# A run of 1,596 extra TensorE products ahead of a decoder step on one core

## The chip, the cores and the metric

One core of a Trainium2 chip runs the whole program. Its engines work side by side and meet at semaphores: TensorE multiplies (PE in the profile, its weight loads PEld), VectorE (DVE) and ScalarE (ACT) do what is elementwise, GpSimd (POOL) a few small things, and SyncE (SP) issues nearly all DMAs. The metric is the device time in microseconds of one execution; lower is better.

## The reference

One layer of a decoder step, for a prompt of 256 tokens and 8 samples of 4 tokens, 288 tokens in all, with a model width of 2048. Everything is in float32.

```python
def _layer(x, c, conv_prefix, chunk, ...):
    mod = (jax.nn.silu(c) @ w_ada + b_ada).reshape(n, N_MOD, 1, D_MODEL)
    sh_m, sc_m, gt_m, sh_f, sc_f, gt_f = [mod[:, i] for i in range(N_MOD)]
    h = _rms(x, g_mix) * (1 + sc_m) + sh_m
    proj = h @ w_in
    b_gate, c_gate, hc, u, v, ga, gb = jnp.split(proj, idx, axis=-1)
    ...
    merged = jax.nn.sigmoid(ga) * (ya @ w_pa) + jax.nn.sigmoid(gb) * (yb @ w_pb)
    x = x + gt_m * (merged @ w_out)
    h2 = _rms(x, g_ffn) * (1 + sc_f) + sh_f
    gate, up = jnp.split(h2 @ w_ffn_in, 2, axis=-1)
    x = x + gt_f * ((jax.nn.silu(gate) * up) @ w_ffn_out)
```

The first product is the conditioning, `silu(c) @ w_ada`; the large ones are those with `w_in`, `w_pa`, `w_pb`, `w_out`, `w_ffn_in` and `w_ffn_out`. The result is `x` under a last norm, with some states of the mixers.

## The kernel before

**Tiles.** Features lie on the 128 partitions and the 288 tokens along a row, so a product has a weight tile of 128x128 as the operand that is loaded and 288 columns (298 for some early ones) that stream through. The output takes the first 288 of the 512 columns of one bank of PSUM. Four banks are called `main` (the names `pm`), three `misc` (`px`), one `ada`.

**Three products for one.** Each float32 operand is split into a high part, rounded to the type FP32R, and a low part, what is left. `triple` (L236) multiplies high by high (L239), high by low (L242) and low by high (L244, or L241 in another order) into one sum. Each product has a weight load of its own in the trace. Weights are split on arrival, the high part on ScalarE (L480), the low one on VectorE (L487, or L258 where the planner of the head does it). The columns that stream through are cut from `slots`, whose FP32R tiles begin seven elements into their buffer (`LEADIN`). The plain FP32 products are those of the conditioning (L412), the sums of squares (L213), the transposes and the spatial mixing.

**Fillers.** `warm(n)` (L600 to L604) multiplies a BF16 tile of ones, `wb`, into the bank `idle`, 288 columns wide, n times; no result is read.

**Order.** TensorE's instructions run in the order in which the Python code calls them. In the head of the program the same holds for ScalarE, VectorE and SyncE. The steps run from a list: 19 fillers, the first conditioning block `a0` (two loads, with 5 fillers between them and 6 inside), then `first_tile`, which makes the first tile of activations out of them (VectorE's L426, L709 and L711, ScalarE's L710), 2 and 6 fillers beside it, then the products of `w0` (L534, L536, L542 and on), with the second conditioning block `a1` among them (L412 again).

**Loads.** All large loads go through one pool of seven buffers, `raw` (`RAW = 7`), in turn: a load waits until what was in its buffer seven loads ago has been read. SyncE issues them in order, at the head `a0`, `w0` and a slice of `x`, `a1`, a slice of `x`, `wK`, `wA` and more of `x`.

Of the kernel before, what the change touches and what calls it, by code (L numbers as in the profile page):

```python
# [8 lines left out]
F32 = mybir.dt.float32  # L9
F32R = mybir.dt.float32r  # L10
# [4 lines left out]
P = 128  # L15
D = 2048
T = 288
# [10 lines left out]
RAW = 7  # L28
# [60 lines left out]
def decoder_kernel(tc, d):  # L89
    nc = tc.nc  # L90
    from contextlib import ExitStack

    with ExitStack() as es:
        def pool(name, bufs=1, **kw):
            return es.enter_context(tc.tile_pool(name=name, bufs=bufs, **kw))

        pc = pool("const")
        pw = pool("wstream")
        pslot = pool("slots", MAIN)
        pkept = pool("kept", KEPT)  # L100
        ptmp = pool("tmp", 5)
        pps = pool("psum", 4, space=bass.MemoryType.PSUM)
        with tc.manual_schedule(engines={nc.tensor.engine}):
            _body(tc, nc, d, pc, pw, pslot, pkept, ptmp, pps)


def _body(tc, nc, d, pc, pw, pslot, pkept, ptmp, pps):
    ids = [0]

    def nm(s):  # L110
        ids[0] += 1
        return f"{s}_{ids[0]}"

    def const(name, shape, dt=F32):
        return pc.tile(shape, dt, tag=name, name=name)
# [12 lines left out]
    def psmain():  # L128
        return pps.tile([P, 512], F32, tag="main", name=nm("pm"), bufs=4)
# [4 lines left out]
    V, A, G, PE, SY = nc.vector, nc.scalar, nc.gpsimd, nc.tensor, nc.sync  # L134
# [16 lines left out]
    x = const("x", [P, 16, T])  # L151
# [215 lines left out]
    class Step:  # L367
        defer = apart = False
        raw = None
# [227 lines left out]
    wb = const("wb", [P, 288], BF16)  # L597
    G.memset(wb, 1.0)
    idle = psmain()
# [200 lines left out]
    def sinkD(m, ps):  # L800
        a = part[m]
        V.tensor_tensor(a, ps[:, :T], a, ALU.add)  # L802
        if 32 <= m < 40:
            gelu2(a)
            if m == 32:
                S["accv"] = SquareSum()
            S["accv"].add(a)
        elif 24 <= m < 32:
            gelu2(a)
            u2[m - 24] = a  # L810
        elif m >= 40:
            A.activation(a, a, AF.Tanh, scale=0.5)
        elif m >= 16:
            mix_conv(m - 16)
# [283 lines left out]
        tail.close()  # L1098


    rh1 = h1.__getitem__
    def at(main, plan):
        out, n = [], 0
        for s in main:
            out.append(s)
            if isinstance(s, Blk):
                n += 1
                out += plan.pop(n, [])
        assert not plan
        return out  # L1110
# [32 lines left out]
    def wD(m0, m1):  # L1143
        return [Blk("wD", i, rh1, sinkD) for i in range(m0 // 2, m1 // 2)]

    first = [Half(n, 0, rh1, lambda j, ps: sinkD(32 + j, ps)) for n in ("wE", "wF")] + wD(36, 40)
# [47 lines left out]
    n = len(steps)  # L1194
# [30 lines left out]
    for s in steps:  # L1225
# [14 lines left out]
        i = pos[id(s)]  # L1240
# [124 lines left out]
```

## Time and profile before

| | |
|---|---|
| median of 2 runs | 1593.24 us (1593.21 to 1593.26) |
| the profiled execution's own time | 1593.33 us |
| its span, first to last instruction | 1591.5 us |
| mean granted TensorE clock | 0.998 of full |
| DMA share of the 16 engines, 0 to 20 and 20 to 40 us | 0.93 and 1.02 |

Times in the trace count from the first instruction. A row of the timeline has the start, the duration, the engine, the line, the operation, what it writes and reads, the shape (128*128 is the weight tile, 128x288 what streams through) and how many alike were merged; in brackets stands the idle time ahead and what ended it. A group's row ends with busy time, the mean of one in ns, and the idle time ahead of the group. A row of the windows has for each engine the busy time and, in brackets, the records that lie in the stretch. TensorE's records overlap: the mean of one says how long it is under way, while the distance from start to start says what it costs.

### The profile page before, as it was taken

The page shows a single profiled execution, that of the slowest core. Times are in us where ns is not written, and L with a number is a line of the kernel's source. Part 1 is how long each engine was busy: PE and PEld are TensorE (multiplying, and loading weights), DVE is VectorE, ACT ScalarE, POOL GpSimd, SP SyncE. Part 2 cuts the span into 40 slices and gives each one's busy share as a digit, 9 for nine tenths or more (in the row PEclk, how much of TensorE's full clock was granted, in tenths as well). Part 3 has the DMA queues.
Part 4 walks back from the last instruction along what each step waited for, and adds up shares of the span by engine and source line. Part 5 has one row for each costly group of instructions (what it writes and reads, how often), then busy time and mean ns, then how long its engine had stood idle before and what let it go on. Part 6 is the DMA issues. An engine that isn't in the chain of part 4 may idle for free.

```text
span 1591.5 us, 31811 instructions
## 1 busy us (share of the span) xinstructions
PE 1581.3 (99%) x12700; PEld 1520.3 (96%) x12700; DVE 1013.9 (64%) x2200; ACT 735.7 (46%) x1366; POOL 21.4 (1%) x65
## 2 busy tenths in 40 slices
PE   9999999999999999999999999999999999999997
PEld 8998999998999989899898999999999999999997
DVE  6676788877755658567844555555555555555565
ACT  6633344643444435356643444444444444444464
POOL 0000000000001000011000000000000000000000
PEclk9999999999999999999999999999999999999999
DMA  9887866777767778784757356453464534645341
GB/s 381 333 322 288 320 243 217 283 280 305 283 232 263 312 290 267 269 295 169 293 180 277 128 182 212 159 177 111 170 232 159 175 121 164 230 159 176 112 165 60
DMA packets 67541, 357.89 MB, mean 225 GB/s; under 512 B 7616, under 2 KB 19264, under 8 KB 37696
## 3 DMA queue, kind: packets, MB, share of 16 engines
q1 hardware_dynamic: 67104, 355.73, 61.2%
q8 instruction: 99, 1.62, 0.4%
q14 instruction: 50, 0.41, 0.1%
q10 hardware_dynamic: 288, 0.13, 0.0%
HBM read 352.74 MB, written 3.09 MB: 224 GB/s over the span
## 4 chain that ended last, share of the span: by engine, by line
PE 99%; DVE 1%; ACT 0%; DVEq 0%; issue 0%; POOL 0%; POOLq 0%
PE pm L239 31%; PE pm L244 30%; PE pm L242 30%; PE ada L412 5%; PE pm L604 0%; DVE st L1079 0%; PE px L242 0%; PE px L239 0%; PE px L244 0%; PE px L213 0%; PE px L911 0%; PE px L910 0%; PE px L857 0%; PE px L1051 0%; PE pm L241 0%; DVE q L620 0%
## 5 line engine op out<-in xcount | busy, mean ns | idle before, releaser
L239 PE MATMUL pm<-s,hi 128*128 128x288 f32 (+1 forms) x3750 | 1095.1, 292 | 0.0
L242 PE MATMUL pm<-s,hi 128*128 128x288 f32 (+1 forms) x3750 | 1090.6, 291 | 0.0
L244 PE MATMUL pm<-s,lo 128*128 128x288 f32 (+1 forms) x3738 | 1088.1, 291 | 0.0
L480 ACT CAST hi<-raw 128x512 fp32r<-128x512 f32 (+1 forms) x963 | 585.2, 610 | 776.8 <-PE pm L242 730.9
L487 DVE TENSOR_TENSOR lo<-raw,hi 128x512 fp32r<-128x512 f32 (+1 forms) x849 | 577.3, 682 | 409.7 <-ACT hi L480 397.6
L239 PEld LDWEIGHTS pm<-s,hi 128*128 128x128 f32 x3750 | 702.1, 187 | 12.7 <-issue 10.4
L242 PEld LDWEIGHTS pm<-s,hi 128*128 128x128 f32 x3750 | 702.2, 187 | 0.1
L244 PEld LDWEIGHTS pm<-s,lo 128*128 128x128 f32 x3738 | 699.9, 187 | 0.0
L258 DVE TENSOR_TENSOR lo<-raw,hi 128x512 fp32r<-128x512 f32 x111 | 74.6, 676 | 28.3 <-ACT hi L480 27.5
L412 PE MATMUL ada<-raw,cs 128*32 128x512 f32 (+2 forms) x1088 | 81.0, 445 | 0.0
L412 PEld LDWEIGHTS ada<-raw,cs 128*32 128x32 f32 x1088 | 29.2, 110 | 40.6 <-issue 37.9
L802 DVE TENSOR_TENSOR s<-pm,s 128x288 f32<-128x288 f32 x72 | 32.8, 456 | 16.6 <-PE pm L244 16.4
L311 ACT CAST s<-t 128x288 fp32r<-128x288 f32 (+1 forms) x76 | 32.9, 433 | 15.4 <-DVE t L834 9.1
L313 DVE TENSOR_TENSOR s<-t,s 128x288 fp32r<-128x288 f32 (+1 forms) x76 | 35.0, 460 | 6.0 <-ACT s L311 5.2
L353 DVE SCALAR_TENSOR_TENSOR x<-pm,mod,x 128x256 f32<-128x256 f32 x79 | 37.5, 475 | 0.0
L1000 DVE SCALAR_TENSOR_TENSOR t<-t,pm 128x288 f32<-128x288 f32 x42 | 19.1, 454 | 19.6 <-PE pm L244 19.6
L794 DVE TENSOR_TENSOR s<-pm,s 128x288 f32<-128x288 f32 x48 | 21.8, 454 | 9.9 <-PE pm L244 9.1
L352 DVE TENSOR_TENSOR t<-pm,mod 128x32 f32<-128x32 f32 x79 | 15.1, 192 | 20.0 <-PE pm L244 19.5
L785 DVE TENSOR_TENSOR s<-s,rb 128x288 f32<-128x288 f32 x48 | 21.6, 449 | 0.0
L181 ACT ACTIVATE t<-x 128x288 f32<-128x288 f32 x29 | 12.9, 444 | 17.7 <-DVE x L356 17.7
L186 DVE TENSOR_TENSOR acc<-acc,t 128x288 f32<-128x288 f32 x33 | 15.0, 455 | 8.2 <-ACT t L181 8.2
L779 DVE SCALAR_TENSOR_TENSOR s<-pm,s 128x256 f32<-128x256 f32 x36 | 17.3, 481 | 2.7 <-PE pm L244 2.7
(170 smaller groups left out, 489.5 us busy)
## 6 DMA issues: line engine op xcount, KB each, us to landing
raw<-in_fi SPq DMA_DIRECT2D x84, 1024.0 KB, 4.8
raw<-in_a SPq DMA_DIRECT2D x56, 1024.0 KB, 4.9
raw<-in_f SPq DMA_DIRECT2D x64, 704.0 KB, 3.9
raw<-in_wD SPq DMA_DIRECT2D x34, 1024.0 KB, 6.9
raw<-in_aE SPq DMA_DIRECT2D x16, 1024.0 KB, 9.6
raw<-in_wo SPq DMA_DIRECT2D x16, 1024.0 KB, 5.7
raw<-in_wC SPq DMA_DIRECT2D x19, 768.0 KB, 4.4
raw<-in_pa SPq DMA_DIRECT2D x8, 1024.0 KB, 9.8
```

Source lines behind the costliest of these rows:

```text
L239: PE.matmul(out, wh, ah, start=first, stop=False)
L242: end_ = PE.matmul(out, wh, al, start=False, stop=turn and last)
L244: end_ = PE.matmul(out, wl, ah, start=False, stop=last)
L258: lows.pop(0)[1]()
L311: A.copy(hi, a)
L313: V.tensor_tensor(lo, a, hi.bitcast(F32), ALU.subtract)
L353: V.scalar_tensor_tensor(x[:, m, :TP], ps[:, :TP], mod[:, gt0 + m, 0:1], x[:, m, :TP], ALU.mult, ALU.add)
L412: PE.matmul(acc[32 * j : 32 * j + 32, h * w // n : (h + 1) * w // n], cs[:, kt, :], self.held[2 * j + h] if self.held else self.raw[:, o : ...
L480: A.copy(hi, self.raw[:, s * 128 : e * 128])
L487: sub()
L794: return V.tensor_tensor(part[m], ps[:, :T], part[m], ALU.add)
L802: V.tensor_tensor(a, ps[:, :T], a, ALU.add)
```

## The change

A function `bench` is added and called once, ahead of the list of steps. VectorE fills a tile of 2048 columns with 0.75; VectorE copies it to one FP32R tile and ScalarE to two more. The four tiles come from the pool of the stream buffers. TensorE then runs 48 fillers and 516 times three products of these constants. They go to `idle` and to three more banks of `main`, and nothing reads them: four times into each bank in turn; to 56 places of one bank (columns 0, 4, ... 220) and to four more (2, 6, 10, 14), six times each; in five orders of banks and places, eight times each, once each product starting its sum and once each adding to what is there; and at nine widths from 288 to 240 columns, eight times each. The columns that stream begin at element 23 or 535 of their tile; the weights begin at multiples of 128 elements, for the low part with 40 added.

```diff
+    def bench():
+        f = pw.tile([P, 2048], F32, tag="raw", name=nm("bench"), bufs=RAW)
+        V.memset(f, 0.75)
+        rs = []
+        for i in range(3):
+            r = pw.tile([P, 2048], F32R, tag="raw", name=nm("benchr"), bufs=RAW)
+            A.copy(r, f) if i else V.tensor_copy(r, f)
+            rs.append(r)
+        r0, r1, r2 = rs
+        outs = [idle] + [psmain() for _ in range(3)]
+
+        def triple_(i, o, out, n=T, first=True):
+            a, b = r2[:, 23 : 23 + n], r2[:, 535 : 535 + n]
+            w, l = (r[:, s + P * (i % 8) : s + P * (i % 8) + P] for r, s in ((r0, 0), (r1, 40)))
+            for q, (x, y) in enumerate(((w, a), (w, b), (l, a))):
+                PE.matmul(out(q)[:, o : o + n], x, y, start=first, stop=True, skip_group_check=True)
+
+        def one(k):
+            return lambda q: outs[k]
+
+        for i in range(48):
+            PE.matmul(idle[:, :T], wb[:, :P], wb, start=True, stop=True)
+        for i in range(4):
+            triple_(i, 0, one(i))
+        for o in range(0, 224, 4):
+            for i in range(6):
+                triple_(i, o, one(0))
+        for o in (2, 6, 10, 14):
+            for i in range(6):
+                triple_(i, o, one(0))
+        for first in (True, False):
+            for i in range(8):
+                triple_(i, 0, one(0), first=first)
+            for i in range(8):
+                triple_(i, 0, one(i % 4), first=first)
+            for i in range(8):
+                triple_(i, 0, lambda q: outs[q], first=first)
+            for i in range(8):
+                triple_(i, 0, lambda q: outs[q % 2], first=first)
+            for i in range(8):
+                triple_(i, 224 * (i % 2), one(0), first=first)
+        for n in (288, 284, 280, 276, 272, 264, 256, 248, 240):
+            for i in range(8):
+                triple_(i, 0, one(0), n)
+
+    bench()
```

On TensorE the new products stand ahead of the 19 fillers with which its program began. This is the start of the changed program's products, behind the last of the 48 fillers (`pm_100` is `idle`; `benchr_103`, `_105` and `_107` are the three FP32R tiles; x2 is two products alike):

```order
L1122 MATMUL pm_100<-wb 128x288
L1116 MATMUL pm_100<-benchr_107,benchr_103 128x288 x2
L1116 MATMUL pm_100<-benchr_107,benchr_105 128x288
L1116 MATMUL pm_109<-benchr_107,benchr_103 128x288 x2
L1116 MATMUL pm_109<-benchr_107,benchr_105 128x288
L1116 MATMUL pm_110<-benchr_107,benchr_103 128x288 x2
L1116 MATMUL pm_110<-benchr_107,benchr_105 128x288
L1116 MATMUL pm_111<-benchr_107,benchr_103 128x288 x2
L1116 MATMUL pm_111<-benchr_107,benchr_105 128x288
```

Nothing stood there before. On ScalarE, whose copies these products wait for, the head of the program before:

```order
L138 DMA t_75<-in_c 128x144
L140 DMA cp_77<-in_cpack 128x112
L164 ACT_TABLE_LOAD
L164 ACTIVATE t_87<-t_75 128x144
L480 CAST hi_244<-raw_109 128x512
L710 ACTIVATE s_251<-x,gm_92 128x256
```

and now:

```order
L138 DMA t_75<-in_c 128x144
L140 DMA cp_77<-in_cpack 128x112
L164 ACT_TABLE_LOAD
L164 ACTIVATE t_87<-t_75 128x144
L1107 CAST benchr_105<-bench_101 128x2048
L1107 CAST benchr_107<-bench_101 128x2048
L480 CAST hi_1851<-raw_1716 128x512
L710 ACTIVATE s_1858<-x,gm_92 128x256
```

The two copies of constants stand between the start of the conditioning and the first split of `w0`. On SyncE, the loads from the rest of `w0` on, before (in brackets the semaphores that a load waits for; those named DMAHW are earlier loads, and `raw_115` and `raw_118` are the two halves of `a1`):

```order
L461 DMA raw_109<-in_w 128x512 [waits DMAHW2_49]
L385 DMA raw_115<-in_a 128x1024 [waits DMAHW3_49]
L385 DMA raw_115<-in_a 128x1024 [waits DMAHW4_49]
L385 DMA raw_118<-in_a 128x1024 [waits DMAHW5_49]
L385 DMA raw_118<-in_a 128x1024 [waits DMAHW6_49]
L155 DMA x<-in_x 128x288 [waits DMAHW7_49]
L463 DMA raw_122<-in_wK 128x768 [waits DMAHW0_49]
```

and now:

```order
L461 DMA raw_1716<-in_w 128x512 [waits DMAHW2_49]
L385 DMA raw_1722<-in_a 128x1024 [waits DMAHW3_49,DVE_49,Activation_49]
L385 DMA raw_1722<-in_a 128x1024 [waits DMAHW4_49]
L385 DMA raw_1725<-in_a 128x1024 [waits DMAHW5_49,PE_49]
L385 DMA raw_1725<-in_a 128x1024 [waits DMAHW6_49]
L155 DMA x<-in_x 128x288 [waits DMAHW7_49]
L463 DMA raw_1729<-in_wK 128x768 [waits DMAHW0_49,PE_49]
```

The first half of `a1` now waits for the copies to have read the float32 constants, the second half and `wK` for TensorE to have read the FP32R ones.

## The prediction

> **What bounds the kernel now.** I read the page first: the shares of the engines, the slices, the chain that ended last. Then the windows, for the spacing of the products, and the timeline of the first 22 us, where the new work is put.
>
> ```profile
> span 1591.5 us, 31811 instructions
> PE 1581.3 (99%) x12700; PEld 1520.3 (96%) x12700; DVE 1013.9 (64%) x2200; ACT 735.7 (46%) x1366; POOL 21.4 (1%) x65
> PEclk9999999999999999999999999999999999999999
> PE 99%; DVE 1%; ACT 0%; DVEq 0%; issue 0%; POOL 0%; POOLq 0%
> ```
>
> TensorE is busy for 99% of the span, its granted clock is full in all forty slices, and 99% of the chain of waits is TensorE itself. So the test for any added work is whether it is on TensorE. What a product costs is its spacing, start to start, since the records overlap. The windows give it for a stretch that holds little else than products 288 wide, and the timeline gives it for 298 columns and for the BF16 fillers.
>
> ```profile
> 1300.00:1580.00 280.00, 280.00 (x2164) 280.00 (x2162) 161.76 (x328) 133.02 (x239) 0.00 (x0) 1.00 0.43 148
> ...
> 12.72 0.29 PE L239 MATMUL px<-s,hi 128*128 128x298 f32 x1
> ...
> 14.59 0.29 PE L242 MATMUL pm<-s,hi 128*128 128x298 f32 x1
> ...
> 1.13 4.74 PE L604 MATMUL pm<-wb 128*128 128x288 bf16 x19 [1.13 <-POOL wb L598]
> 5.80 1.24 PE L412 MATMUL ada<-raw,cs 128*32 128x64 f32 x64
> 6.97 0.79 PE L604 MATMUL pm<-wb 128*128 128x288 bf16 x5
> ...
> 9.70 1.15 PE L604 MATMUL pm<-wb 128*128 128x288 bf16 x8
> 11.01 0.40 PE L534 MATMUL pm<-s,hi 128*128 128x298 f32 x1 [0.16 <-ACT s L710]
> ...
> L239 PE MATMUL pm<-s,hi 128*128 128x288 f32 x3626 | 1058.0, 292 | 0.0
> ...
> L604 PE MATMUL pm<-wb 128*128 128x288 bf16 x49 | 9.6, 348 | 1.1 <-POOL wb L598 1.1
> ```
>
> 280 us hold 2164 products, of which two straddle the edges: 280/2162 = 0.1295 us each. Between 12.72 and 14.59 us lie 14 steps of 298-wide products: 1.87/14 = 0.1336 us. Ten columns more cost 4.1 ns, so 0.41 ns a column: the width sets the spacing there, on a fixed part of 129.5 - 288 x 0.41 = 11 ns. A merged row of n records lasts n - 1 spacings and one record, and the groups give the record (292 ns for a product, 348 on average for a filler, near 290 for one at full speed). So the first 19 fillers are spaced (4.74 - 0.35)/18 = 0.244 us, the last 8 (1.15 - 0.29)/7 = 0.123 us: TensorE starts at half speed and has reached full speed by the row at 6.97, whose five are spaced (0.79 - 0.29)/4 = 0.125 us.
>
> **What the change adds on TensorE.** 48 fillers and, from `triple_`, three products a call. The calls: 4 that touch each of four banks, 56 places x 6, 4 places x 6, two passes of five orders x 8, and nine widths x 8: 4 + 336 + 24 + 80 + 72 = 516 calls, 1548 products. Of these 9 x 8 x 3 = 216 belong to the widths, and 1332 are 288 wide. Nothing can hide them: TensorE runs in program order, they stand ahead of everything, and no other engine ends the span.
>
> The 288-wide ones are the kernel's own product in shape and type, with the same two weights for three streams (high, high, low), and the L239 rows stand for them. Sum: 1332 x 0.1295 = 172.5 us.
>
> The 216 narrower ones have 288, 284, 280, 276, 272, 264, 256, 248 and 240 columns, 24 each, 267.6 on average. By 0.41 ns a column that is 129.5 - 20.4 x 0.41 = 121.1 ns, 26.2 us in all. No FP32R row of this trace is narrower than 288. The other end, no gain from narrowness, is 216 x 0.1295 = 28.0 us. A floor from the weight loads shows in the products of one column:
>
> ```profile
> 41.31 0.83 PE L213 MATMUL px<-ones,q 128*128 128x1 f32 x6 [0.20 <-DVE q L620]
> ...
> 426.89 0.60 PE L857 MATMUL px<-cp,s 128*128 128x128 f32 x4
> ...
> L857 PE MATMUL px<-cp,s 128*128 128x128 f32 x16 | 2.4, 272 | 0.0
> ...
> L213 PE MATMUL px<-ones,q 128*128 128x1 f32 x6 | 0.8, 254 | 0.2 <-DVE q L620 0.2
> ```
>
> Six products of one column take 0.83 us, (0.83 - 0.26)/5 = 0.114 us apart, where one column would need next to nothing: a new set of 128 weights is not taken faster than about 0.11 us. The line through the two widths meets that near 245 columns, so only the 240s could touch it, for a few ns on 24 products. I take 26.2 us.
>
> **The place in the bank and the order of the banks.** No row writes 288 columns anywhere but at a bank's start. The nearest is L857: four products that write at columns 0, 128, 256 and 384 of one bank stand (0.60 - 0.27)/3 = 0.11 us apart, each as the next. I price the place at nothing. Above, 1,086 products lie off the start, and if such a place cost what ten columns cost (4.1 ns), that is 4.5 us. Below, if it brought the spacing down to that of the BF16 fillers (0.123), 1,086 x 6.5 ns = 7 us less. For the order of banks the four L534, four L536 and four L542 change bank with every product, the first four starting a sum, the others adding; this group gives the spacing:
>
> ```profile
> 11.65 0.69 PE L536 MATMUL pm<-s,lo 128*128 128x298 f32 x4
> 12.19 0.69 PE L542 MATMUL pm<-s,hi 128*128 128x298 f32 x4
> ```
>
> (0.69 - 0.29)/3 = 0.133 us in both, the 298-wide spacing within one bank. So the five orders, adding or overwriting, cost nothing extra.
>
> [...]
>
> **When they start, and the head behind them.** The operands are constants: a VectorE memset of 2048 columns, one VectorE copy, two ScalarE copies.
>
> ```profile
> 4.67 0.32 ACT L164 ACTIVATE t<-t 128x144 f32<-128x144 f32 x1 [1.72 <-DMA t<-in_c]
> ...
> L480 ACT CAST hi<-raw 128x512 fp32r<-128x512 f32 x892 | 549.4, 618 | 714.4 <-PE pm L242 673.0 <-PE pm L244 10.4 <-DVE lo L487 6.6
> ...
> L480 ACT CAST hi<-raw 128x256 fp32r<-128x256 f32 x5 | 2.0, 407 | 1.6 <-DVE s L785 0.9 <-PE pm L242 0.6
> ```
>
> ScalarE's queue holds them behind L164, which waits for a DMA to 4.67 and ends at 4.99. 512 columns take 618 ns, 256 take 407: 0.82 ns a column, so 2048 take 1.88 us, and two are done at 8.8. VectorE's memset and copy are done before that, and what they push back there (L165 and L166, wanted at 5.80 before) is now wanted only 200 us later. Meanwhile TensorE runs the 48 fillers: 21 at 0.244 from 1.13 to some 6.2, then 27 at 0.123, to 9.5. So the first product starts at about 9.6, held by the fillers rather than by ScalarE, and the last ends at 9.6 + 172.5 + 26.2 = 208.3.
>
> Behind it stands the old head, unchanged: 19 fillers, now at full speed, 19 x 0.123 = 2.3 us with 0.1 for the change of type, and then what took from 5.80 to 11.01 before, 5.2 us, less 0.1 as its first 64 products ran partly at half speed. L534 comes at 208.3 + 2.4 + 5.1 = 215.8 in place of 11.01. What follows keeps its order. The shift is 204.8 us.
>
> **The loads that wait.** Four of the seven stream buffers now hold the constants, so the second half of `a1` and all behind it on SP's queue (a slice of x, `wK`, `wA`) issue only at 208.3, when the last product has read its operands. Before:
>
> ```profile
> 6.65 2.88 SPq L385 DMA_DIRECT2D raw<-in_a  x4
> 9.63 0.37 SPq L155 DMA_DIRECT2D x<-in_x  x1
> 10.28 0.33 SPq L463 DMA_DIRECT2D raw<-in_wK  x1
> ...
> 17.31 1.15 PE L412 MATMUL ada<-raw,cs 128*32 128x64 f32 x64
> ...
> 19.13 0.51 ACT L480 CAST hi<-raw 128x384 fp32r<-128x384 f32 x1 [3.63 <-DVE gm L709]
> ```
>
> That half of `a1` is the last two of the four at 6.65, some 8.3, 2.7 us ahead of L534; now it is 7.5 us ahead. It is wanted at 17.31, 6.3 behind L534, so 13.8 us after its issue; `wK` is wanted at 19.13, 8.1 behind L534, so some 14 after its own. A DMA of `a1` takes 6.9 us to land, one of `wA`, the slowest at the head, 10.0:
>
> ```profile
> raw<-in_a SPq DMA_DIRECT2D x8, 512.0 KB, 6.9
> raw<-in_wA SPq DMA_DIRECT2D x6, 512.0 KB, 10.0
> ```
>
> So I cost this at nothing: the cover is the head's 7.5 us. Without it up to 8 us would show. The earlier loads (`a0`, `w0`, half of `a1`) land under the products, yet TensorE gains little, as it stood still for only parts of a microsecond between 11 and 40 us.
>
> **Sum.** The profiled execution took 1593.33 us, 1.83 more than its span, and the median is 1593.24, 0.09 less. 1591.5 + 204.8 = 1796.3 for the span, and 1798.1 for the time; I say 1798.0.
>
> **Rivals.**
> - Narrow FP32R products run as plain FP32 ones, below a width that this trace doesn't show. A plain FP32 product leaves two records (L911, eight products, 16 records):
>
> ```profile
> L911 PE MATMUL px<-s,s 128*128 128x128 f32 x16 | 3.1, 275 | 0.0
> ...
> 287.17 4.50 PE L412 MATMUL ada<-raw,cs 128*32 128x512 f32 x40
> ...
> L412 PE MATMUL ada<-raw,cs 128*32 128x512 f32 x576 | 64.7, 594 | 0.0
> ```
>
>   At 512 columns four such records lie side by side, so 40 take ten steps: (4.50 - 0.59)/9 = 0.434 us, 0.85 ns a column. Two records of 244 columns are 0.415 us, against 0.112: 0.3 us more on each product concerned. If that is the two narrowest widths, 48 products, 14.5 us, which makes 1812.5. Against it: nothing in this trace hints at such a width; for it: the nine widths go well below what the kernel uses. Chance 0.09.
> - The FP32R products, freed of other engines' traffic, space as the BF16 fillers, 0.1225: 187.8 in place of 198.7, so 1787. Against it: the 0.1295 is as steady in the quiet stretch from 1300 to 1580 as elsewhere. 0.05. [...]
> - The loads behind the products don't come in time, or a place in the bank costs: 3 to 8 us, 1801 to 1806. 0.05.
> - TensorE's clock drops under the dense stream: at 0.244 a product 1548 x 0.115 = 178 us more, 1976. The kernel is itself such a stream at full clock; 0.01.
> - The other side, no slower: the products never run, since no result is read. They stand in the program as built, and the records of before hold 49 fillers (L604), whose results are not read either. With fillers and copies alone L534 would come at 17 and the time at 1599. It decides as soon as fewer than 32/0.13 = 246 of the 1548 are left. 0.01.
>
> **How the numbers follow.** The forecast has 0.79: 1798, and 1793 to 1803 by its own terms (the width's two ends, the place, a clock that rises 1.5 us earlier or later). 1790 to 1813 takes in the stall and the narrow rival and leaves out the BF16 spacing, the clock and the removal. 2% of the time, 32 us, is about what a measurement can tell from no change; all cases but the last lie far beyond it: slower 0.98, same 0.01, faster 0.01.
>
> **What would show it.** L1116 with 1548 records (a few per cent may be missing) and a spacing of 0.1295 at all 60 places and in all ten orders; widths that fall by 0.41 ns a column and flatten near 0.11; the first L1116 at 9.6, L534 at 216; `a1`'s second half issued when L1116 ends, and TensorE not waiting for it; the rest a copy of before. Wrong would be: a group of L1116 with another spacing, two records to a narrow product, or waits for a DMA in the 30 us behind.

## The result, and the profile after

The changed kernel takes 1797.51 us (1797.15 to 1797.87), against 1593.24: a ratio of 1.1282, 95% interval 1.1264 to 1.1300, so 204.3 us slower. The forecast was 1798.0.

The page of the changed kernel shows the same picture as before with one group more. The columns of the fifth row are shares of the chain that ended last, by engine and line:

```profile
span 1795.4 us, 35011 instructions
PE 1785.4 (99%) x14296; PEld 1723.4 (96%) x14296; DVE 1018.0 (57%) x2202; ACT 739.5 (41%) x1368; POOL 20.8 (1%) x65
PEclk9999999999999999999999999999999999999999
DMA  2000398786577767777766663554446443554341
PE pm L239 27%; PE pm L244 27%; PE pm L242 27%; PE pm L1116 11%; PE ada L412 5%; PE pm L604 0%; DVE st L1079 0%; DMA t<-in_c 0%; ACT benchr L1107 0%; PE px L242 0%; PE px L239 0%; PE px L244 0%; PE px L213 0%; PE px L911 0%; PE px L910 0%; PE px L857 0%
```

TensorE has 14296 - 12700 = 1596 records more, just the 48 fillers and 1,548 products: none was dropped, and none was run as two. The span and TensorE's busy time are both some 204 us longer. The DMA row shows three of forty slices without any traffic: those are the loads that waited for the products to end.

The timeline of the changed kernel, TensorE alone, at the start and the end of the new part:

```profile
8.87 71.31 PE L1116 MATMUL pm<-benchr,benchr 128*128 128x288 f32 x548
...
208.01 2.50 PE L604 MATMUL pm<-wb 128*128 128x288 bf16 x19
210.44 1.10 PE L412 MATMUL ada<-raw,cs 128*32 128x64 f32 x64
...
215.51 0.80 PE L534 MATMUL pm<-s,hi 128*128 128x298 f32 x4 [0.16 <-ACT s L710]
```

The new products take 208.01 - 8.87 = 199.1 us, L534 comes at 215.51 instead of 11.01, and what follows it lasts 1795.4 - 215.5 = 1579.9 us (before 1591.5 - 11.0 = 1580.5).

What each place, order and width costs is read from the same timeline in stretches that lie within one kind. A row gives the start, the duration of all, and their number; the spacing is the duration less one record (0.29 us at 288 columns), by the number less one. First a stretch of 536 products at places from column 0 on, then the four places 2, 6, 10 and 14, then the five orders that start a sum each time, then the five that add:

```profile
10.54 69.64 PE L1116 MATMUL pm<-benchr,benchr 128*128 128x288 f32 x536
...
141.08 9.49 PE L1116 MATMUL pm<-benchr,benchr 128*128 128x288 f32 x72
150.41 15.85 PE L1116 MATMUL pm<-benchr,benchr 128*128 128x288 f32 x121
165.97 15.72 PE L1116 MATMUL pm<-benchr,benchr 128*128 128x288 f32 x120
```

The spacings are 0.1296, 0.1296, 0.1297 and 0.1297 us. By the start times of the single products, each of the 60 places has 0.1296 to 0.1297 and each of the ten orders 0.1295 to 0.1297. So neither the place in a bank, nor the change of banks, nor adding in place of starting a sum has a price. The widths:

```profile
184.76 3.13 PE L1116 MATMUL pm<-benchr,benchr 128*128 128x284 f32 x23
193.93 3.02 PE L1116 MATMUL pm<-benchr,benchr 128*128 128x272 f32 x23
199.90 2.75 PE L1116 MATMUL pm<-benchr,benchr 128*128 128x256 f32 x22
205.43 2.52 PE L1116 MATMUL pm<-benchr,benchr 128*128 128x240 f32 x21
```

With records of 0.29, 0.29, 0.28 and 0.27 us that is 0.129, 0.124, 0.118 and 0.112 us: falling with the width, the last at the floor that the prediction read from the one-column products.

### The profile page after: what moved, and what is told of

Its sections match the earlier page's. It is cut to its first block, busy times and chain, and to the rows that moved or that the text cites. A ratio compares the mean times of both kernels' runs of the same rounds, so it can differ in the third digit from the quotient of the medians.

```text
span 1795.4 us, 35011 instructions
## 1 busy us (share of the span) xinstructions
PE 1785.4 (99%) x14296; PEld 1723.4 (96%) x14296; DVE 1018.0 (57%) x2202; ACT 739.5 (41%) x1368; POOL 20.8 (1%) x65
## 4 chain that ended last, share of the span: by engine, by line
PE 99%; DVE 1%; ACT 0%; DMA 0%; DVEq 0%; issue 0%
PE pm L239 27%; PE pm L244 27%; PE pm L242 27%; PE pm L1116 11%; PE ada L412 5%; PE pm L604 0%; DVE st L1079 0%; DMA t<-in_c 0%; ACT benchr L1107 0%; PE px L242 0%; PE px L239 0%; PE px L244 0%; PE px L213 0%; PE px L911 0%; PE px L910 0%; PE px L857 0%
## 5 line engine op out<-in xcount | busy, mean ns | idle before, releaser
L1116 PEld LDWEIGHTS pm<-benchr,benchr 128*128 128x128 f32 x1548 | 199.1, 187 | 0.4 <-ACT benchr L1107 0.4
L1116 PE MATMUL pm<-benchr,benchr 128*128 128x288 f32 (+7 forms) x1548 | 199.3, 290 | 0.1
L426 DVE STREAM_TRANSPOSE ev<-ada 128x512 f32<-128x512 f32 (+2 forms) x9 | 4.8, 537 | 225.6 <-PE ada L412 225.6
L412 PE MATMUL ada<-raw,cs 128*32 128x512 f32 (+2 forms) x1088 | 80.7, 444 | 0.0
L412 PEld LDWEIGHTS ada<-raw,cs 128*32 128x32 f32 x1088 | 29.0, 110 | 40.4 <-issue 38.1
```

The lines of the kernel that those rows point to most:

```text
L412: PE.matmul(acc[32 * j : 32 * j + 32, h * w // n : (h + 1) * w // n], cs[:, kt, :], self.held[2 * j + h] if self.held else self.raw[:, o : ...
L1116: PE.matmul(out(q)[:, o : o + n], x, y, start=first, stop=True, skip_group_check=True)
```

## The experiments

Each is an edit of the changed kernel. Where a kernel was timed, a time of the kernel before stood beside it, 1593.2 to 1593.3.

**What the products alone cost.** All but three of them are left out:

```diff
-        for i in range(4):
-            triple_(i, 0, one(i))
...
+        for k, r in enumerate(rs):
+            PE.matmul(outs[k + 1][:, :T], r0[:, :P], r[:, 23 : 23 + T], start=True, stop=True)
```

> Left out: the 1,548 products of constants but three, one for each tile; the 48 fillers, the copies and the four buffers stay. Theory (the time is the products' spacing, 199.0 us from 8.87 to 207.9, and a start of some 6 us): the products run from 8.87 to 9.3, 19 fillers follow for 2.4 us, L534 comes near 16.9 in place of 11.0, and the time is near 1599, so that the 1,545 products alone are worth 198 to 199 us. Rival (the held loads or the buffers taken cost something of their own, that hid in the 204 us): over 1602.

It took 1599.27 us (1598.90 to 1600.05). The 1,545 products are worth 1797.51 - 1599.27 = 198.2 us, as expected, and fillers, copies and taken buffers 6.0 us. In this execution full speed came later, 6.3 us into the span in place of 4.5, so the 48 fillers ran to 9.7 in place of 8.8, and L534 came at 17.42.

**What the fillers ahead of them do.** The 48 are left out:

```diff
-        for i in range(48):
-            PE.matmul(idle[:, :T], wb[:, :P], wb, start=True, stop=True)
```

> Left out: the 48 fillers ahead of the products. In the changed kernel the first product waits for ScalarE's copies to 8.87, 0.38 us behind the last filler. Theory: it still starts at 8.87, but at half speed, with a spacing of 0.24 us until the clock is granted in full some 3.5 to 5 us later; that costs 1.7 to 2.5 us, so about 1799.5. Rival (the fillers and not the copies hold the start, the clock does not matter here): the same time within 0.5 us or less.

It took 1799.48 us (1799.32 to 1799.64), 2.0 more. TensorE's timeline of this kernel at the start:

```profile
8.65 5.17 PE L1116 MATMUL pm<-benchr,benchr 128*128 128x288 f32 x20 [8.65 <-ACT benchr L1107]
13.83 5.36 PE L1116 MATMUL pm<-benchr,benchr 128*128 128x288 f32 x40
```

The first 20 products are (5.17 - 0.29)/19 = 0.257 us apart, the next 40 0.130. The start is ScalarE's, with and without fillers; what the fillers buy is full speed at that moment, 0.130 us in place of 0.257.

**Whether the held loads cost anything.** The constants lie in slots instead of stream buffers:

```diff
-        f = pw.tile([P, 2048], F32, tag="raw", name=nm("bench"), bufs=RAW)
+        f = tmp()
...
+        a, b = slot(F32R), slot(F32R)
+        w, l = (
+            pslot.tile([P, o + 256], F32R, tag="s", name=nm("s"), padded_shape=[P, PITCH])[:, o:] for o in (0, 8)
+        )
```

> The constants lie in four tiles of the activation slots in place of four stream buffers, so that no load waits for the products and all seven buffers are filled long before the first conditioning product. The weights repeat after two tiles in place of eight; everything else of the products is the same. Theory (the loads held behind the products were covered by the 7.5 us of the head): the smaller copies end before the fillers, the first product comes 0.3 us earlier, and the time is 1797.0, within 1 us of the changed kernel. Rival (TensorE waited for loads behind the products): 3 to 8 us faster, 1790 to 1794.

It took 1798.18 us (1798.14 to 1798.21), 0.7 more than the changed kernel, where 0.5 less was expected: a small miss, and on the side away from the rival. The first product came at 8.92, not earlier, since the fillers lasted that long in this execution, and the products themselves took 0.5 us longer from their other places. The loads, all there ahead of time, brought nothing, so in the changed kernel they cost nothing.

**How wide the cover is.** The prediction called the head's 7.5 us, from the last product to L534, the cover of the held loads. Of the fillers behind the products, the 30 in front of and within `a0` are left out:

```diff
-    a0[1].half = lambda: warm(6)
...
-    steps = [Do(lambda: warm(19)), a0[0], Do(lambda: warm(5)), a0[1]]
+    steps = [a0[0], a0[1]]
```

> Left out: the fillers of the old head that follow the products, 19 ahead of the first conditioning block, 5 ahead of its second load and 6 in it. Theory: they cost 30 times 0.123 us and some changes of type, about 4 us, and the held loads still come in time, as the second half of a1 is wanted some 9.7 us behind its issue in place of 13.5: 1793.5. Rival (these fillers cover the held loads): under 1.5 us gained, and TensorE waits for a DMA in the 20 us behind L534.

The two executions took 1794.48 and 1798.81 us. In the profiled one, which is the faster, L534 came 4.1 us earlier, as expected, but TensorE lost 1.2 us behind it. The same kernel again:

> The same kernel as the one without the old head's fillers, to see which of its two times holds. Theory (the 1.2 us in which TensorE stood still in the midst of the second a1 block are the price of going into the crowded loads early, and the slower execution had one more stretch at half speed): most runs near 1794.5, the idle time ahead of L412 there again. Rival (that idle time was chance): 1793.3 and no such idle time.

Four executions took 1794.77, 1796.81, 1796.88 and 1798.47 us. The expected idle time ahead of L412 was there again; "most runs near 1794.5" was a miss, with one of four there. TensorE's timeline and then the windows of this second profile (the last three columns of a windows' row are the granted clock, the DMA share and GB/s):

```profile
218.03 0.98 PE L412 MATMUL ada<-raw,cs 128*32 128x64 f32 x54
220.87 0.47 PE L412 MATMUL ada<-raw,cs 128*32 128x64 f32 x10 [1.86 <-issue]
221.28 0.62 PE L239 MATMUL pm<-s,hi 128*128 128x298 f32 x1
221.69 0.45 PE L241 MATMUL pm<-s,lo 128*128 128x298 f32 x1
```

```profile
212.00:219.00 7.00, 7.00 (x154) 6.42 (x153) 4.49 (x12) 3.61 (x10) 0.00 (x0) 1.00 0.98 321
219.00:221.10 2.10, 0.24 (x12) 0.23 (x10) 0.00 (x0) 0.00 (x0) 0.00 (x0) 1.00 1.02 413
221.10:224.50 3.40, 3.40 (x23) 3.25 (x15) 2.53 (x11) 1.43 (x3) 0.00 (x0) 0.50 1.02 415
```

TensorE stands still for 1.86 us after 54 of the 64 products of the second `a1` block, while the DMA engines are full (1.02). Just then the granted clock falls to 0.50 for 3.4 us: the pause costs 1.86 us for itself, and behind it products of 298 columns start 0.25 us apart, where the changed kernel has 0.13. It is not the block's own data, since each half of the block has its load and the second half begins with the 33rd product.

**Whether the crowded loads make that pause.** Both edits together, the constants in the slots and the fillers left out:

> Both edits together: constants in the activation slots, so that no load waits for the products, and none of the 30 fillers behind them. Theory (TensorE stood still in the midst of the second a1 block because the held loads crowded the DMA engines there): no idle time ahead of L412, the whole 4.1 us gained on the kernel with the slots, 1794.0. Rival (the idle time belongs to the short fillers being gone, whatever the loads do): about 1795.3, idle time there again.

It took 1793.85 us (1793.33 to 1793.98), four executions, and the block runs through:

```profile
218.42 1.10 PE L412 MATMUL ada<-raw,cs 128*32 128x64 f32 x64
219.45 0.40 PE L239 MATMUL pm<-s,hi 128*128 128x298 f32 x1
```

From 212 to 219 us the DMA share is 0.16 here, where it was 0.98 to 1.00 in the two profiles with the pause. So the pause comes from the loads that were held and then all issued at once.

What TensorE lacked in it, the waits don't name ("issue": no semaphore), but the trace's DMA packets point at its instructions. On the queue that the page calls instruction (q8), packets of 16 KB follow one another under the added products about every 16.6 us, the time of 128 products, so they look like TensorE's program. Both profiles with the pause stop ahead of the same product, the 55th. The last such packet before it came from 217.32 to 218.23 us for the pause that ended at 219.79, and from 218.54 to 219.49 for the one that ended at 220.87. With both edits it came from 215.24 to 216.56, well ahead of that product at 219.18. That the crowded DMA engines delayed TensorE's instructions fits all three profiles, but no experiment changed that alone.

**What sets a product's spacing: the width and the type.** Other widths, then BF16 and plain FP32 operands, in place of the places and orders:

```diff
+        for n in (512, 448, 384, 352, 320, 304, 288, 240, 224, 192, 128, 64):
+            for i in range(8):
+                triple_(i, 0, one(0), n)
```

> In place of the places and orders: FP32R products of 512 to 64 columns, 24 of each width, then BF16 products of 512, 288, 240 and 128 columns, 24 each, then plain FP32 ones of 512 and 288. Theory A (a fixed part of some 9.5 ns for each FP32R product, and a floor of the weight loads near 112 ns): 512 columns every 222 to 223 ns, 384 every 169, 224 to 64 every 112. Theory B (the extra lies in weight loads that hardly fit under 288 columns, and goes away where there is room): 512 columns every 216 ns as BF16, 384 every 162.5, and the same floor. Rival (narrow FP32R products run as plain FP32 ones): 224 to 64 columns cost more than 240. BF16: 216, 122.5, 102.5 and 56 ns if a product's columns set it, not under about 110 if the weight loads do. The whole time is no measure here.

TensorE's timeline of this kernel, FP32R (L1116) and BF16 (L1132):

```profile
12.93 5.26 PE L1116 MATMUL pm<-benchr,benchr 128*128 128x512 f32 x22
23.52 4.00 PE L1116 MATMUL pm<-benchr,benchr 128*128 128x384 f32 x22
...
44.10 2.51 PE L1116 MATMUL pm<-benchr,benchr 128*128 128x224 f32 x21
...
52.07 2.40 PE L1116 MATMUL pm<-benchr,benchr 128*128 128x64 f32 x20
...
61.52 2.86 PE L1132 MATMUL pm<-benchb 128*128 128x288 bf16 x22
64.46 2.42 PE L1132 MATMUL pm<-benchb 128*128 128x240 bf16 x22
66.92 1.34 PE L1132 MATMUL pm<-benchb 128*128 128x128 bf16 x21
```

A record takes 0.39 us at 512 columns, 0.33 at 384 and 0.27 to 0.28 at 224 and 64; of BF16 it takes 0.286 at 288, 0.266 at 240 and 0.22 at 128. So FP32R has 512 columns every 0.232 us, 384 every 0.174, 224 and 64 every 0.112, and BF16 288 every 0.1226, 240 every 0.1026, 128 every 0.056. BF16's 512 columns come every 0.216 us by their start times, once the clock, at half from 54.7 to 58.1 us, is full again. The rival of two records is gone: under 240 columns nothing doubles, and the spacing is flat near the 0.11 us that the prediction took for the weight loads. The price that it gave that rival was right: a plain FP32 product leaves two records in this run, 0.2425 us apart at 288 columns. Neither A (0.222) nor B (0.216) has the 512 right: what an FP32R product takes beyond BF16's spacing grows with its columns, from 7 ns at 288 to some 16 at 512.

**Whether the start of the columns plays a part.** 288 columns from other starts, and weights from others:

```diff
+        for at in (*range(0, 17), 20, 23, 24, 28, 31):
+            for i in range(8):
+                triple_(i, at, 0, 40)
```

> In place of the places and orders: 288-wide FP32R products, 24 each, whose columns begin at elements 0 to 16, 20, 23, 24, 28 and 31 of their tile, and whose weights begin at several elements past a multiple of 128 for the high and for the low part. Theory (what the added products cost is what they cost in the kernel because columns and weights begin as they do there): the start that the added products use, element 23, gives 129.6 ns, and some others give more, by up to 10 ns. Rival: the start plays no part, 129.6 ns everywhere within 0.2. If some start gives under 127 ns, the kernel itself could use it. The whole time is no measure here.

TensorE's timeline for the starts at elements 1, 9 and 23:

```profile
16.13 3.00 PE L1116 MATMUL pm<-benchr,benchr 128*128 128x288 f32 x21
...
41.67 3.15 PE L1116 MATMUL pm<-benchr,benchr 128*128 128x288 f32 x22
...
70.42 2.89 PE L1116 MATMUL pm<-benchr,benchr 128*128 128x288 f32 x21
```

That is 0.1355, 0.136 and 0.130 us; all starts lie between 0.130 and 0.136, those of the weights move it by up to 3 ns, and none gives under 0.127. So the start plays a part, and element 23, at which the added products begin, is the best of those tried with their weights. The kernel's own columns begin at element 7 of their slots. At element 7 of this run's tile a product takes 0.131 us with these weights and 0.130 with both weights at multiples of 128, and it took 0.1300 in the slots of the third experiment above. Nothing here makes either kernel faster.

**When the clock is taken back.** Long stretches of narrow FP32R products, and behind each 48 of 288 columns:

```diff
+        for n in (64, 128, 192, 224, 240):
+            for i in range(48):
+                triple_(i, 0, one(0), n)
+            for i in range(16):
+                triple_(i, 0, one(0))
```

> In place of the places, orders and widths: FP32R products of 64, 128, 192, 224 and 240 columns, 144 of each width, and behind each width 48 of 288 columns that show the clock. With the widths before, TensorE's clock fell to half for 3.4 us just behind 5.3 us of products of 128 and 64 columns, without any idle time. Theory (products that are spaced by their weight loads count as little work, and the clock is taken back): the 288-wide ones behind the 64-column stretch of 16 us, and behind the 128-column one, begin with a spacing of 0.24 us or more; behind 224 and 240 columns they are at 0.1296 from the start. Rival (the fall came from the change to BF16 operands, or by chance): full clock throughout. The whole time is no measure here.

Half of the theory held: behind the 64-column stretch the 288-wide products begin 0.24 us apart, behind the 128-column one 0.130. The windows within the 64-column stretch and the 128-column one:

```profile
12.00:15.00 3.00, 3.00 (x30) 3.00 (x28) 0.00 (x0) 0.00 (x0) 0.00 (x0) 1.00 0.55 214
16.00:39.00 23.00, 23.00 (x110) 23.00 (x110) 0.00 (x0) 0.00 (x0) 0.00 (x0) 0.50 0.00 1
...
48.00:63.00 15.00, 15.00 (x137) 15.00 (x136) 0.00 (x0) 0.00 (x0) 0.00 (x0) 1.00 0.00 1
```

About 3 us into the 64-column products the granted clock is 0.50, with TensorE busy throughout by its records, and their spacing grows from 0.112 to 0.21 us; at 128 columns and above it stays full.

## Why the prediction was right

It was right in the time and in each large term. The start was 0.7 us early, the products 0.4 us longer and the rest 0.6 us shorter than forecast, which makes the span 1795.4 where 1796.3 was forecast. That the median is 1797.51, only 0.5 under the forecast, owes something to the second execution, 0.7 us slower than the profiled one.

- **The products.** 1,548 counted, 1,548 found; 198.7 us forecast, 199.1 measured. The 288-wide term rests on 0.1295 us from the quiet stretch of the kernel before, and the added products, of the same type and width and each with a weight load, have 0.1296. The prediction did not weigh the start of the columns, which matters by up to 6 ns a product, some 9 us in all. The two starts, element 7 and element 23, came out alike, and that was luck; why they did was not shown.
- **The narrow ones.** Forecast 26.2 us on a straight line, measured 26.4 from 181.65 to the end. The floor at 0.11 us, read from one-column products, is where they flatten (0.112). That it is one of 128 new weights as such was not shown: BF16 products, each with other weights than the one before, came every 0.056 us at 128 columns. All nine widths lie within some 2 ns of the line.
- **Place and order** at nothing: shown at all 60 places and ten orders.
- **The start.** Forecast at 9.6, held by the fillers; it was 8.87, held by ScalarE. This step failed: by the trace's record of the clock full speed came 4.5 us into the span where 6.2 was taken (there the fillers' spacing goes from 0.240 to 0.1225 us), the fillers were done at 8.8, and ScalarE's second copy ended at 8.82 as forecast. The changed kernel's timeline, ScalarE and TensorE's weight loads:

```profile
5.14 3.68 ACT L1107 CAST benchr<-bench 128x2048 fp32r<-128x2048 f32 x2
...
8.87 0.69 PEld L1116 LDWEIGHTS pm<-benchr,benchr 128*128 128x128 f32 x5 [0.38 <-ACT benchr L1107]
```

- **The head behind them.** From the first of the 19 fillers to L534 7.5 us, as forecast (2.4 + 5.1).
- **The rest** was taken as unchanged and came out 0.6 us shorter. 0.3 of it is a wait of TensorE for VectorE's L720 in the second tile, which stood in the kernel before and is not among the waits now. The other 0.3 was not traced; executions of the kernel before differ by 0.8 among themselves.
- **The held loads** at nothing: right, with little to spare. With 4.1 of the 7.5 us of cover gone, TensorE pauses for 1.2 us in one profile, and in the other for 1.9 us with 3.4 us at half clock behind. The pause is not a wait for the load that the prediction named, so the cover was needed for a reason that it did not have. Its "up to 8 us" for no cover at all was not tested.
- **The rivals.** Two records to a narrow product, the BF16 spacing, a lower clock and dropped products are each excluded by a row above, and so is a price of the place. The 187.8 us given for the BF16 spacing is 1332 x 0.1225 + 216 x 0.114: the spacing of the fillers in the kernel before, and the same less 20.4 columns at 0.41 ns. The added products have 0.1296 where BF16's 288 columns have 0.1226. The stall exists, but only with part of the cover gone.

## What to carry to other kernels

On TensorE, busy for 99% of the span here, the added products cost their count times their start-to-start spacing: 1,548 took 199.1 of the 204.3 us. Take the spacing from rows that agree in type, width and start of the operands: BF16's at the same 288 columns is 0.1226 us, FP32R's 0.1296. The fillers of a head were a cover in two ways here: without the 48, the first 20 products came 0.257 us apart in place of 0.130, and without the 30, TensorE paused for 1.2 and 1.9 us under the held loads. Before removing fillers, see what is issued at once behind them. A benchmark within the kernel must keep the clock up: products of 64 columns, or a pause of 1.9 us, were followed here by products at a granted clock of 0.50.

## What the runs showed of the hardware

- FP32R products came no closer than 0.111 to 0.112 us, from 240 columns down to 64, where BF16 came every 0.056 us at 128 columns.
- FP32R's spacing for 288 columns differed with the element at which the columns begin: 0.130 to 0.136 us.
- About 3 us into a dense stream of 64-column FP32R products the granted clock fell to 0.50, without a gap in TensorE's records; under 15 us of 128-column ones it stayed at 1.00. Behind the pause of 1.86 us it was 0.50 for 3.4 us.
- With the DMA engines full (share 0.98 to 1.02), TensorE stood still for 1.2 and 1.9 us without a semaphore to wait for, ahead of the same product in both profiles; with a share of 0.16 ahead of that product it did not.
